# A hybrid attention block on one core: compression blocks, a q projection and the final gain moved to other places in the engines' queues

## The chip, the cores and the metric

The kernel runs on one core of a Trainium2 chip. That core has a matrix engine (TensorE, PE in the profile; PEld is its weight load), a vector engine (VectorE, DVE), a scalar engine (ScalarE, ACT), a general engine (GpSimd, POOL) and a queue that issues most transfers (SyncE, SP). Each engine works off its own queue in order, and they wait for each other by semaphores. The metric is the device time of one execution in microseconds (us); less is better. Three runs of the kernel before took 855.98, 856.62 and 858.67 us, so its median is 856.62 us.

## What is computed

The reference is one decoder block on x (512 tokens, 2048 features): a root-mean-square norm, one projection into queries, keys, values and gates, two kinds of attention, a SiLU gate, an output projection with a residual, and a last norm.

```python
h = _rmsnorm(x, norm_g[l]);  proj = h @ w_in[l]
kc = _compress(_rope(kca), cmp_k_pos, cmp_k_w1, cmp_k_w2)     # blocks of 32 tokens, stride 16
vc = _compress(vca, cmp_v_pos, cmp_v_w1, cmp_v_w2)            # silu((blocks + pos) @ w1) @ w2
o_cmp = attention(qa, kc, vc);  o_sel = selected blocks;  o_win = window of 512
o_a = g0 * o_cmp + g1 * o_sel + g2 * o_win                    # 8 heads of 128
o_b = banded attention, window 128, with sinks                # 16 heads of 64
x = x + concat(o_a * silu(za), o_b * silu(zb)) @ w_out
out = _rmsnorm(x, final_g)
```

`final_g` multiplies every column of the output, after each row has been divided by its root mean square.

## The kernel before

Every large product is made in three matmuls (`mm3`, L89): a float32 operand is split into a rounded high part and the low rest, and high by high, high by low and low by high are added up in PSUM. For a weight this split is `load_unit` (L60): SP issues a transfer of up to 128x1024 into `raw`, ACT rounds it to `whi` (L68), VectorE subtracts to get `wlo` (L69). `whi` and `wlo` have three buffers each, so ACT starts a new one only when the PE has finished with the one three units back. In the output projection `halves` and `split_to` (L632, L634) do the same.

The stages that the change touches, in order of time:

- **Opening and key loop** (L145, L241). The opening makes the keys and values that will be compressed (PSUM banks 0 to 3, `acc0`). The key loop over eight units of `w0[1]` makes the other keys (banks 4 to 7). Into its units, behind the `wlo` of each (`issue_after(last["lo"])` holds VectorE's part of a block behind that instruction), a list `work` puts one job each: `kv_evac` of the compressed keys (L179, three VectorE products with the rope tables and a sum), four `blocks_part` (L190) for them, and `kv_evac` of the compressed values (one VectorE product). A `blocks_part` is one VectorE sum with the position table into `ff` (L194), one ACT copy into the high half of F (L195) and one VectorE difference into the low half (L196).
- **First value loop** (L263): values from `w1s`, and the hidden layer of key compression from F0 (`compress_unit`, L199, which has a weight unit of its own and eight matmuls, L204 and L205).
- **Second value loop** (L292): nine rounds. Round u makes values and gates from `w2s` (408 columns; banks 4, 5, 2, 3) and, one round later, a unit of value compression from F1. F0 and F1 share one buffer (`tag="F"`), so the four `blocks_part` of F1 (L296) stand in round 0, when the PE has read F0 for the last time.
- **Evacuation of v** (L305): per tile of 128 tokens ACT scales and copies out of PSUM (L272, L273, L307), VectorE scales the gates (L308), POOL makes a low part (L274). Then the second compression layer, and then the heads. The first head begins with `proj(wz[0])`, two units of 24 matmuls of 512 columns, and goes on with the projection of its gate.
- **Output projection** (L684 to the end). The 2048 output columns go in four parts of 512. Part 0 is plain. Parts n = 1 to 3 work on sums and differences of quarter blocks: `product` with the operands named p, 22, 12, u, 21, q, w, where some weights are sums of two quarters. `summed` (L761) loads one quarter and adds the other to it with a transfer that POOL issues (L765); `add_to` (L769) adds a third quarter on VectorE (L772); `plus` (L784) adds results into `xs[n]`. The gain `final_g` is multiplied in by `times_g` (L663), a 128x512 product on POOL (L665), for parts 0 to 2; part 3 takes it in `final` (L670). Twelve such products run: those of part 1 and then of part 0 at the end of n = 1, those of part 2 within n = 2. A square with a row sum on ACT (`square`, L656) must have read a tile before its gain is multiplied in.

The order of the work on each engine is not written by hand: the program is made with `schedule_with_timeline_sim=True`, so a planner that simulates the engines takes instructions in the order of the program as their inputs and buffers come free, and `issue_after` puts bounds on it. The order that comes out is fixed at build time.

Of the kernel before, what the change touches and what calls it, by code (L numbers as in the profile page):

```python
# [10 lines left out]
F32 = mybir.dt.float32  # L11
# [22 lines left out]
def hybrid_block(ctx, tc, xT, xtm, w0, w1s, w2s, wz, wkb, wo0, wos, cw1, cw2, cpos, rope, tabs, sinks, gT, fg, out):  # L34
# [54 lines left out]
    def mm3(ps, ah, al, bh, bl, first, last, go_on=False):  # L89
        pe.matmul(ps, ah, bh, start=first, stop=False, skip_group_check=go_on)  # L90
        pe.matmul(ps, ah, bl, start=False, stop=False, skip_group_check=go_on)  # L91
        pe.matmul(ps, al, bh, start=False, stop=last, skip_group_check=go_on)  # L92
# [92 lines left out]
            dve.tensor_tensor(out=kvts[b][:, g, 0:S], in0=ps, in1=rstdb, op=ALU.mult)  # L185

    def blocks_tile(b):
        return s0.tile([P, 32, P], F32R, name=f"F{b}", tag="F")

    def blocks_part(Fb, b, g, half):  # L190
        ff = tmp("ff").rearrange("p (a b) -> p a b", b=32)
# [42 lines left out]
                    lo[:, j * width:(j + 1) * width], first, k == KT - 1 and (t % 2 == 1 or not shared))  # L234

    F0 = blocks_tile(0)
    work = [lambda g=g: kv_evac(0, g) for g in range(2)]
    work += [lambda g=g, half=half: blocks_part(F0, 0, g, half) for half in range(2) for g in range(2)]
    work += [lambda g=g: kv_evac(1, g) for g in range(2)]
    acc1 = [bank(4 + i) for i in range(4)]  # L240
    for u in range(KT // 2):  # L241
        hi, lo = load_unit(w0[1, :, u], 1024)
        with tc.issue_after(last["lo"]):
            work[u]()
        for j in range(2):
# [40 lines left out]

    for t in range(NQ):
        v_evac(t, 0, sacc[t])
    F1 = blocks_tile(1)
    sacc2 = [bank(t) for t in (4, 5, 2, 3)]  # L290
    vacc = bank(0)
    for u in range(9):  # L292
        if u < 8:
            tok_chunk(w2s, 408, [a[:, 0:408] for a in sacc2], False, u)
        if u == 0:
            for half in range(2):  # L296
                for g in range(2):
                    with tc.issue_after(last["lo"]):
                        blocks_part(F1, 1, g, half)
        else:  # L300
            compress_unit(F1, 1, u - 1, vacc)
        if u in (3, 5):
            with tc.issue_after(last["lo"]):
                k_evac(1, u // 5)
    for t in range(NQ):  # L305
# [21 lines left out]

    yt = [None] * 16
    ypair = []

    def proj(src):
        ps = psp.tile([P, S], F32, name="pj", tag="pj")
        for u in range(2):
            hi, lo = load_unit(src[:, u], 1024)
            for j in range(8):
                k = 8 * u + j
                mm3(ps, hi[:, j * P:(j + 1) * P], lo[:, j * P:(j + 1) * P], xh[:, k, :], xl[:, k, :], k == 0,
                    k == KT - 1)
        return ps

    def z_evac(ps):
        zr = wk.tile([P, S], F32, name="zr", tag="t2", bufs=1)
# [130 lines left out]

    for h in range(8):
        if h == 0:
            qh, ql = q_evac(proj(wz[0]), cosA, sinA)
        st = z_evac(proj(wz[8 + h]))
        cur = (qh, ql)
        attn_a(h, *cur, st)
        if h < 7:  # L480
            qh, ql = q_evac(proj(wz[h + 1]), cosA, sinA)
# [180 lines left out]

    def times_g(n, t):  # L663
        v = xs[n][t // 2][:, t % 2, :]
        pool.tensor_tensor(out=v, in0=v, in1=fgt[n // 2][:, (n % 2) * 512:(n % 2) * 512 + 512], op=ALU.mult)  # L665

    def pre_norm(t, k):
        dve.tensor_reduce(out=rs2[:, t, 0:1], in_=ssq[:, t, 0:k], axis=AX.X, op=ALU.add)
# [57 lines left out]
    for n in range(1, 4):  # L726
# [69 lines left out]
        if n < 3:  # L796
# [5 lines left out]
            product(bx, [halves(c) for c in ch], "u", True)  # L802
            plus(gg, gg, bx)
            plus(xa[1], xa[1], gg)
            r12 = [load(raw(), 1, g) for g in range(2)]
            if n == 1:
                load_gain()
# [1 line left out]
            plus(xb[1], xb[1], bb)  # L809
            plus(jj, jj, bb)  # L810
            plus(xb[0], xb[0], jj)
            add_to(ch, r12)
            product(bx, [halves(c) for c in ch], "q", False)
            plus(xb[0], xb[0], bx)
            for t in range(2):
                square(ssq[:, t, n + 1:n + 2], xs[n][0][:, t, :])
                times_g(n, t)
            s1 = summed(rw, 2, 3)
            product(bc, [halves(c) for c in s1], "w", True)
            plus(xa[1], xa[1], bc)  # L820
            for t in range(2, 4):
                square(ssq[:, t, n + 1:n + 2], xs[n][1][:, t - 2, :])
                times_g(n, t)
            if n == 1:
                for t in range(NQ):
                    times_g(0, t)
        else:
            by = psf1.tile([P, S], F32, name="oa", tag="oa").rearrange("p (t c) -> p t c", c=256)
            bxt = [bx, by]
            add_to(ch, r22)  # L830
            u5 = [halves(c) for c in ch]
            for t in range(2):
                product(bxt[t], u5, "u", True, (t,))
            for t in range(2):
                plus(xa[1][:, t, :], xa[1][:, t, :], bxt[t][:, t, :])
            plus(xa[1], xa[1], gg)
            r12 = [load(raw(), 1, g) for g in range(2)]
            product(bb, [halves(r) for r in r12], "21", False)
            plus(xb[1], xb[1], bb)
# [97 lines left out]
```

## Time and profile before

| | |
|---|---|
| median of 3 runs | 856.62 us |
| the profiled execution, its own time | 857.36 us |
| its span, first to last instruction | 855.3 us |
| busy PE | 835.8 us, 98% |
| busy VectorE / ACT / POOL | 591.1 / 405.1 / 112.6 us |
| mean granted PE clock | 0.994 |
| opening and key loop | 0 to 97 us |
| first / second value loop | 97 to 127 / 127 to 175 us |
| heads | 175 to about 700 us |
| output projection | about 670 to 850 us |

A busy PE is not a PE at its peak: matmuls overlap, and the end of one is modelled. Where the PE waits, though, the profile shows a gap and names what ended it. The rows of a timeline give start, duration, engine, line, and in brackets the idle time before the instruction with what it waited for.

### The profile page before, as it was taken

Reading aid. Unit: us, or ns where it says so; the run is one execution under the profiler, and the core shown is the slowest. Engines: PE = TensorE matmul, PEld = TensorE weight load, DVE = VectorE, ACT = ScalarE, POOL = GpSimd, SP = SyncE. Lnnn points to the kernel's source line nnn. Section 1 sums busy time; section 2 is a strip of 40 time slices with the busy share of each in tenths; the row PEclk is TensorE's granted clock in tenths of the full one; section 3 lists DMA queues with packets and bytes.
Section 4 is the critical chain, followed back from the end, with each engine's and each line's share of the span. In section 5 each row is a group of like instructions: output and inputs, shape, how many; then the busy total and the mean of one; then the engine's idle time right before and its main releaser. Section 6 shows DMA issues by size and latency. Waiting matters only on the chain.

```text
span 855.3 us, 12745 instructions
## 1 busy us (share of the span) xinstructions
PE 835.8 (98%) x4776; PEld 729.6 (85%) x4776; DVE 591.1 (69%) x1232; ACT 405.1 (47%) x845; POOL 112.6 (13%) x83
## 2 busy tenths in 40 slices
PE   9999998999999999999999999999999999899994
PEld 8788898978888888888888888888888788899994
DVE  6829476655675565775766877777767898767765
ACT  6723255443454443444443554544444737243536
POOL 4500001021110110110111201011101000430310
PEclk9999999999999999999999999999999999999998
DMA  9632274632212122121221221222222139696975
GB/s 324 207 120 87 86 227 134 192 107 91 75 50 75 58 66 74 60 65 61 89 74 51 92 79 54 90 82 72 68 83 75 49 99 310 160 276 162 260 164 197
DMA packets 33773, 101.40 MB, mean 119 GB/s; under 512 B 4016, under 2 KB 4016, under 8 KB 33712
## 3 DMA queue, kind: packets, MB, share of 16 engines
q1 hardware_dynamic: 30400, 90.90, 32.6%
q0 software_dynamic: 2016, 7.34, 5.0%
q10 hardware_dynamic: 1296, 2.36, 0.8%
q8 instruction: 37, 0.61, 0.3%
q14 instruction: 24, 0.20, 0.1%
HBM read 96.39 MB, written 4.19 MB: 118 GB/s over the span
## 4 chain that ended last, share of the span: by engine, by line
PE 88%; DMA 4%; DVE 3%; ACT 2%; issue 1%; SPq 0%; POOL 0%; ACTq 0%; DVEq 0%; POOLq 0%
PE pj L91 16%; PE pj L90 16%; PE pj L92 16%; PE bank L90 4%; PE bank L91 4%; PE bank L92 4%; PE sp L412 3%; PE oa L91 3%; PE oa L90 3%; PE oa L92 3%; DMA ch<-wos 2%; PE tp L447 2%; PE tp L582 1%; DMA raw<-wos 1%; PE op L456 1%
## 5 line engine op out<-in xcount | busy, mean ns | idle before, releaser
L90 PE MATMUL pj<-xh,whi 128*128 128x512 f32 x560 | 222.1, 397 | 0.7 <-ACT whi L68 0.7
L91 PE MATMUL pj<-xl,whi 128*128 128x512 f32 x560 | 222.3, 397 | 0.0
L92 PE MATMUL pj<-xh,wlo 128*128 128x512 f32 x560 | 221.8, 397 | 0.5 <-DVE wlo L69 0.5
L68 ACT ACTIVATE whi<-raw 128x1024 fp32r<-128x1024 f32 (+2 forms) x129 | 125.0, 972 | 159.9 <-PE pj L91 79.6
L69 DVE TENSOR_TENSOR wlo<-raw,whi 128x1024 fp32r<-128x1024 f32 (+2 forms) x130 | 151.4, 1170 | 68.9 <-ACT whi L68 67.9
L92 PEld LDWEIGHTS pj<-xh,wlo 128*128 128x128 f32 x560 | 105.4, 188 | 23.5 <-DVE wlo L69 1.0
L90 PEld LDWEIGHTS pj<-xh,whi 128*128 128x128 f32 x560 | 105.4, 188 | 22.9 <-ACT whi L68 1.0
L91 PEld LDWEIGHTS pj<-xl,whi 128*128 128x128 f32 x560 | 105.5, 188 | 22.5 <-issue 0.9
L353 POOL TENSOR_TENSOR t<-t,t 128x512 f32<-128x512 f32 x17 | 34.9, 2054 | 400.4 <-DVE t L97 384.9
L91 PE MATMUL oa<-wlo,yh 128*128 128x256 f32 (+1 forms) x208 | 62.3, 300 | 0.5 <-DVE wlo L634 0.5
L90 PE MATMUL oa<-whi,yh 128*128 128x256 f32 (+1 forms) x208 | 61.9, 299 | 0.6 <-ACT yh L629 0.6
L92 PE MATMUL oa<-whi,yl 128*128 128x256 f32 (+1 forms) x208 | 61.6, 299 | 0.0
L382 DVE TENSOR_TENSOR pl<-tp,ph 128x512 fp32r<-128x512 f32 x56 | 37.7, 685 | 34.3 <-ACT ph L381 34.1
L381 ACT ACTIVATE ph<-tp 128x512 fp32r<-128x512 f32 x56 | 32.4, 594 | 53.3 <-PE tp L447 43.5
L91 PE MATMUL bank<-wlo,xh 128*128 128x256 f32 (+1 forms) x128 | 40.1, 315 | 2.4 <-DVE wlo L69 2.4
L90 PEld LDWEIGHTS oa<-whi,yh 128*128 128x128 f32 x208 | 39.1, 188 | 2.1 <-ACT yh L629 0.8
L91 PEld LDWEIGHTS oa<-wlo,yh 128*128 128x128 f32 x208 | 39.2, 188 | 2.0 <-DVE wlo L634 0.7
L92 PEld LDWEIGHTS oa<-whi,yl 128*128 128x128 f32 x208 | 39.2, 188 | 1.4
L92 PE MATMUL bank<-whi,xl 128*128 128x256 f32 (+1 forms) x128 | 39.8, 313 | 0.0
L561 ACT ACTIVATE ttb<-ttb,mnb 128x256 f32<-128x256 f32 (+1 forms) x64 | 30.1, 471 | 20.2 <-DVE mnb L554 19.6
L90 PE MATMUL bank<-xh,whi 128*128 128x512 f32 x96 | 37.4, 400 | 0.0
L90 PE MATMUL bank<-whi,xh 128*128 128x256 f32 (+1 forms) x128 | 36.9, 316 | 0.5 <-ACT whi L68 0.5
(277 smaller groups left out, 1734.2 us busy)
## 6 DMA issues: line engine op xcount, KB each, us to landing
raw<-wz SPq DMA_DIRECT2D x64, 512.0 KB, 3.6
raw<-cw SPq DMA_DIRECT2D x16, 512.0 KB, 3.8
raw<-wos SPq DMA_DIRECT2D x14, 512.0 KB, 4.7
rw<-wos SPq DMA_DIRECT2D x12, 512.0 KB, 5.1
xr<-xT SPq DMA_DIRECT2D x16, 256.0 KB, 5.4
raw<-w SPq DMA_DIRECT2D x8, 512.0 KB, 3.7
raw<-wo SPq DMA_DIRECT2D x8, 512.0 KB, 3.7
raw<-w SPq DMA_DIRECT2D x15, 256.0 KB, 4.7
```

Source lines behind the costliest of these rows:

```text
L68: act.activation(hi[:, :width], raw[:, :width], AF.Copy)
L69: last["lo"] = dve.tensor_tensor(out=lo[:, :width], in0=raw[:, :width], in1=hi[:, :width].bitcast(F32), op=ALU.subtract).ins
L90: pe.matmul(ps, ah, bh, start=first, stop=False, skip_group_check=go_on)
L91: pe.matmul(ps, ah, bl, start=False, stop=False, skip_group_check=go_on)
L92: pe.matmul(ps, al, bh, start=False, stop=last, skip_group_check=go_on)
L353: pool.tensor_tensor(out=t1, in0=t1, in1=t2, op=ALU.add)
L381: act.activation(ph, tp, AF.Copy)
L382: dve.tensor_tensor(out=pl, in0=tp, in1=ph.bitcast(F32), op=ALU.subtract)
L412: pe.matmul(sp[:, a:b], qq[:, qs], kk[g][:, ko:ko + b - a], start=pi == 0, stop=pi == 2)
L447: pe.transpose(tp[:, e * 256 + i * P:e * 256 + i * P + P], views[2 * i + w][2][:, kt * P:(kt + 1) * P], ident)
L456: pe.matmul(oc, VL[:, kt, w, vs], ph[:, es], start=False, stop=False)
L561: act.activation(tv, tv, AF.Exp, bias=mn[:, e, v:v + 1], scale=-1.0, accum_out=dn[:, e, v:v + 1])
```

## The change

Three edits, all of order and place; the arithmetic is the same.

1. F0 and F1 get a buffer each. All eight `blocks_part` and all four `kv_evac` go into the key loop: unit 0 and 1 the two key evacuations, unit 2 both value evacuations, units 3 and 4 the four parts of F0, units 5, 6 and 7 one, two and one part of F1. The second value loop has eight rounds, and compression runs in the same round as the projection.
2. `proj(wz[0])` stands ahead of the evacuation of v, and the first head takes its result.
3. `times_g` runs on VectorE, each behind the last `wlo` that the program has issued, and at other places: part 0 in n = 2 (two tiles behind the sum that follows product u, two ahead of `add_to(ch, r12)`), parts 1 and 2 in n = 3 (two ahead of `add_to(ch, r22)`, four behind the sums that follow product u, two behind the loads for product 12).

```diff
     def blocks_tile(b):
-        return s0.tile([P, 32, P], F32R, name=f"F{b}", tag="F")
+        return s0.tile([P, 32, P], F32R, name=f"F{b}")
...
     F0 = blocks_tile(0)
-    work = [lambda g=g: kv_evac(0, g) for g in range(2)]
-    work += [lambda g=g, half=half: blocks_part(F0, 0, g, half) for half in range(2) for g in range(2)]
-    work += [lambda g=g: kv_evac(1, g) for g in range(2)]
+    F1 = blocks_tile(1)
+    kv = [lambda b=b, g=g: kv_evac(b, g) for b in range(2) for g in range(2)]
+    bp = [lambda Fb=Fb, b=b, g=g, half=half: blocks_part(Fb, b, g, half)
+          for b, Fb in enumerate((F0, F1)) for half in range(2) for g in range(2)]
+    work = [kv[:1], kv[1:2], kv[2:], bp[0:2], bp[2:4], bp[4:5], bp[5:7], bp[7:]]
...
         with tc.issue_after(last["lo"]):
-            work[u]()
+            for job in work[u]:
+                job()
...
-    F1 = blocks_tile(1)
...
-    for u in range(9):
-        if u < 8:
-            tok_chunk(w2s, 408, [a[:, 0:408] for a in sacc2], False, u)
-        if u == 0:
-            for half in range(2):
-                for g in range(2):
-                    with tc.issue_after(last["lo"]):
-                        blocks_part(F1, 1, g, half)
-        else:
-            compress_unit(F1, 1, u - 1, vacc)
+    for u in range(8):
+        tok_chunk(w2s, 408, [a[:, 0:408] for a in sacc2], False, u)
+        compress_unit(F1, 1, u, vacc)
...
+    q0 = proj(wz[0])
     for t in range(NQ):
         v_evac(t, 1, sacc2[t])
...
-            qh, ql = q_evac(proj(wz[0]), cosA, sinA)
+            qh, ql = q_evac(q0, cosA, sinA)
...
     def times_g(n, t):
         v = xs[n][t // 2][:, t % 2, :]
-        pool.tensor_tensor(out=v, in0=v, in1=fgt[n // 2][:, (n % 2) * 512:(n % 2) * 512 + 512], op=ALU.mult)
+        with tc.issue_after(last["lo"]):
+            dve.tensor_tensor(out=v, in0=v, in1=fgt[n // 2][:, (n % 2) * 512:(n % 2) * 512 + 512], op=ALU.mult)
...
             plus(xa[1], xa[1], gg)
+            if n == 2:
+                for t in range(2):
+                    times_g(0, t)
             r12 = [load(raw(), 1, g) for g in range(2)]
...
             plus(xb[0], xb[0], jj)
+            if n == 2:
+                for t in range(2, 4):
+                    times_g(0, t)
             add_to(ch, r12)
...
                 square(ssq[:, t, n + 1:n + 2], xs[n][0][:, t, :])
-                times_g(n, t)
...
                 square(ssq[:, t, n + 1:n + 2], xs[n][1][:, t - 2, :])
-                times_g(n, t)
-            if n == 1:
-                for t in range(NQ):
-                    times_g(0, t)
         else:
...
+            for t in range(2):
+                times_g(1, t)
             add_to(ch, r22)
...
             plus(xa[1], xa[1], gg)
+            for t in range(2):
+                times_g(1, 2 + t)
+                times_g(2, 2 + t)
             r12 = [load(raw(), 1, g) for g in range(2)]
...
             s2 = summed(raw, 0, 2)
+            for t in range(2):
+                times_g(2, t)
             plus(xa[1], xa[1], bc)
```

More of the change, by code (lines that the diff above doesn't have):

```diff
@@ L304, in hybrid_block, with proj @@
                 k_evac(1, u // 5)
+    def proj(src):
+        ps = psp.tile([P, S], F32, name="pj", tag="pj")
+        for u in range(2):
+            hi, lo = load_unit(src[:, u], 1024)
+            for j in range(8):
+                k = 8 * u + j
+                mm3(ps, hi[:, j * P:(j + 1) * P], lo[:, j * P:(j + 1) * P], xh[:, k, :], xl[:, k, :], k == 0,
+                    k == KT - 1)
+        return ps
+    q0 = proj(wz[0])
     for t in range(NQ):
@@ L329, in hybrid_block @@
     ypair = []
[L331 to L339, printed above, removed]
     def z_evac(ps):
```

## The prediction

> **What bounds the kernel now.** I read the page first (busy shares), then the list of waits for the PE alone, then the timeline around each wait.
>
> ```profile
> span 855.3 us, 12745 instructions
> PE 835.8 (98%) x4776; PEld 729.6 (85%) x4776; DVE 591.1 (69%) x1232; ACT 405.1 (47%) x845; POOL 112.6 (13%) x83
> ```
>
> The PE is busy for 98% of the span. The change takes no matmul away, so it can win only what the PE now loses in waits and in a lowered clock, and it loses wherever it makes the PE wait anew. The waits of the PE, each with total, count and longest in us:
>
> ```profile
> PE oa L91 <- DVE wlo L634: 3.1, 3, 2.4
> PE bank L91 <- DVE wlo L69: 2.4, 1, 2.4
> PE pj L90 <- ACT whi L68: 0.7, 1, 0.7
> PE pj L92 <- DVE wlo L69: 0.5, 1, 0.5
> PE bank L90 <- ACT whi L68: 0.5, 1, 0.5
> ```
>
> These five rows are nearly all of it, and each of the three edits stands beside one place: the two with `bank` (L69, L68) lie in the second value loop, the two with `pj` at the first q projection, and the 2.4 us of L634 in the output projection. What follows takes the places in turn.
>
> **Edit 1, the blocks of F1.** What VectorE and ACT do at the start of the second value loop, and the PE's wait there:
>
> ```profile
> 126.47 4.87 DVE L194 TENSOR_TENSOR ff<-kvt,pos 128x512 f32<-128x512 f32 x4
> 131.26 3.17 DVE L69 TENSOR_TENSOR wlo<-raw,whi 128x816 fp32r<-128x816 f32 x2
> 134.35 2.48 DVE L196 TENSOR_TENSOR F<-ff,F 128x512 fp32r<-128x512 f32 x4
> ```
>
> ```profile
> 132.81 0.46 PE L91 MATMUL bank<-wlo,xh 128*128 128x408 f32 x1 [2.44 <-DVE wlo L69]
> 133.11 0.35 PE L92 MATMUL bank<-whi,xl 128*128 128x408 f32 x1
> 133.30 0.34 PE L91 MATMUL bank<-wlo,xh 128*128 128x408 f32 x1
> ...
> 139.38 1.00 PE L90 MATMUL bank<-whi,xh 128*128 128x408 f32 x4 [0.46 <-ACT whi L68]
> ```
>
> ```profile
> 138.45 0.88 ACT L68 ACTIVATE whi<-raw 128x816 fp32r<-128x816 f32 x1 [2.81 <-PE bank L204]
> ```
>
> Four sums L194 take VectorE from 126.47 to 131.3, and the `wlo` that the PE needs is behind them: 2.44 us. The second wait is a consequence. The `whi` at 138.45 waits for a buffer that the PE gives back only with the compression matmuls (L204), which need F1, finished at 136.8: 0.46 us. With F1 built in the key loop both causes are gone, and compression of round 0 becomes work that the PE can take at once. Late next is the chain of key compression, since bank 3 of the new accumulators is taken by it until `kct` is read; it now also waits behind the F1 work, so I expect it earlier, not later. Gain: 2.9 us (2.44 + 0.46); at worst none of it, if evacuations on ACT keep `whi` late.
>
> What the key loop then has to carry: four L194 and four L196 more, and four ACT copies L195. Groups of VectorE from 60 to 98 us (busy, mean ns, idle before), and the copies (ns):
>
> ```profile
> L69 DVE TENSOR_TENSOR wlo<-raw,whi 128x1024 fp32r<-128x1024 f32 (+1 forms) x8 | 8.7, 1084 | 11.8 <-ACT whi L68 11.8
> L194 DVE TENSOR_TENSOR ff<-kvt,pos 128x512 f32<-128x512 f32 x4 | 4.0, 1046 | 0.0
> L196 DVE TENSOR_TENSOR F<-ff,F 128x512 fp32r<-128x512 f32 x4 | 2.5, 672 | 0.0
> ```
>
> ```profile
> L195 ACT ACTIVATE F<-ff x8: 620/636/641, 75.2 to 132.4; 128x512 fp32r<-128x512 f32 x8
> ```
>
> Four parts of F cost VectorE 4.0 + 2.5 = 6.5 us, and it idles 11.8 us in this stretch waiting for `whi`, while the PE waits nowhere. So the added 6.5 us cost nothing; the cover is that idle time, and what finds none of it is paid in full. There is one tight spot: the two value evacuations L185 (products of the size of L196, 2 x 0.67 = 1.3 us) now stand in unit 2, ahead of the `wlo` of unit 3, and that one is just in time:
>
> ```profile
> 69.13 1.23 DVE L69 TENSOR_TENSOR wlo<-raw,whi 128x1024 fp32r<-128x1024 f32 x1
> ```
>
> ```profile
> 70.50 0.63 PE L92 MATMUL bank<-xh,wlo 128*128 128x512 f32 x2
> 70.97 0.63 PE L92 MATMUL pj<-xh,wlo 128*128 128x512 f32 x2
> ```
>
> It ends at 70.36 and is read at 70.50. If L185 goes ahead, up to 1.3 us could open. But the planner has put L90 and L91 of four banks ahead of that L92, work without `wlo`, and the second half of the unit has four more such pairs (two matmuls from 70.50 to 70.97 make 0.23 us each, eight 1.9 us). I take 0 and keep 0 to 1.3 us for the range; a gain isn't to be had where the PE does not wait.
>
> **Edit 2, the q projection ahead of the evacuation of v.** ACT's queue at the end of the second value loop:
>
> ```profile
> 171.52 0.47 ACT L272 ACTIVATE vt<-bank,rstd 128x256 f32<-128x256 f32 x1 [1.20 <-PE bank L92]
> ...
> 174.57 1.10 ACT L68 ACTIVATE whi<-raw 128x1024 fp32r<-128x1024 f32 x1
> ```
>
> Evacuating copies fill ACT from 171.52 to 174.57 ahead of the first `whi` of the projection, and ACT had been idle for 1.20 us before them. The two `pj` waits, 0.7 and 0.5 us, are this `whi` and its `wlo`. Moved ahead, the `whi` needs only a buffer; with compression in the same round, the buffer three units back belongs to the compression unit before the last projection, freed 24 matmuls of 0.19 us (133.11 to 133.30), 4.6 us, and a compression unit before the loop's end. Gain 1.2 us. The evacuations then run under 48 matmuls of `pj`; at 0.23 us each that is 11 us of cover for a little over 3 us of ACT. What is queued behind: the value compression chain (two tiny PE steps), on which the freeing of the opening's buffers and so the evacuation of q0 hang. If its first PE step is put behind the whole of q0, the gate's projection, another 11 us, is its cover. I take 0; no row shows a wait there, the nearest are the two `pj` rows, so 0 to 1.2 us.
>
> **Edit 3, the gain on VectorE.** POOL, VectorE and PE around the largest wait:
>
> ```profile
> 729.22 6.99 POOL L665 TENSOR_TENSOR xs<-xs,late 128x512 f32<-128x512 f32 x4 [9.95 <-DMA late<-fg]
> ```
>
> ```profile
> 730.73 2.10 DVE L634 TENSOR_TENSOR wlo<-ch,whi 128x1024 fp32r<-128x1024 f32 x1 [2.83 <-ACT whi L633]
> 732.75 4.54 DVE L772 TENSOR_TENSOR ch<-ch,rw 128x1024 f32<-128x1024 f32 x2
> ...
> 737.81 2.35 DVE L634 TENSOR_TENSOR wlo<-ch,whi 128x1024 fp32r<-128x1024 f32 x2
> ```
>
> ```profile
> L772 DVE TENSOR_TENSOR ch<-ch,raw 128x1024 f32<-128x1024 f32 x2 | 2.4, 1218 | 0.0
> L785 DVE TENSOR_TENSOR late<-late,e 128x512 f32<-128x512 f32 x2 | 1.4, 683 | 0.0
> ```
>
> ```profile
> 736.26 0.38 PE L90 MATMUL oa<-whi,uh 128*128 128x256 f32 x1
> 739.08 0.39 PE L91 MATMUL oa<-wlo,uh 128*128 128x256 f32 x1 [2.43 <-DVE wlo L634]
> ```
>
> While POOL multiplies (729.22 to 736.2), a `wlo` takes 2.10 us and the two `ch` sums 4.54 us; the same sums take 1.22 us each a little later. Without POOL's products VectorE saves 0.9 + 2.1 = 3.0 us ahead of the `wlo` that the PE waits 2.43 us for, so that wait goes, with about half a microsecond to spare. And the PE pays for it twice (a stretch, its length, PE, PEld, VectorE, ACT and POOL busy, then the granted clock):
>
> ```profile
> 735.00:740.00 5.00, 2.57 (x19) 2.23 (x18) 5.00 (x5) 3.07 (x3) 2.00 (x2) 0.97 0.60 179
> 740.00:745.00 5.00, 5.00 (x33) 5.00 (x32) 2.77 (x5) 1.06 (x1) 0.96 (x2) 0.69 0.91 160
> ```
>
> At a clock of 0.69 it loses 5 x 0.31 = 1.55 us behind the wait. Gain 2.43 + 1.55 = 4.0 us; at least nothing. The Trainium skill (TensorE: Matmul & The Clock Gate, Part 1) has the clock fall only after an idle window of about 3.4 us, by which 2.43 us would not do it and edit 3 would be worth 2.4 us. The trace shows the fall here, and none behind the equally long wait at 132.81 (the PE steps there are 0.19 us again from 133.11 on), so I go by the rows.
>
> Against it stand twelve products on VectorE, 0.68 us each by L785: 8.2 us. Four are in n = 2:
>
> ```profile
> 775.00:815.00 40.00, 40.00 (x340) 40.00 (x339) 30.57 (x33) 18.24 (x24) 10.34 (x10) 1.00 0.86 235
> ```
>
> The PE never waits there and VectorE has 9.4 us free for 2.7 us; I take 0 (at worst 2.7 us). Eight are in n = 3, where VectorE still has holes:
>
> ```profile
> 818.27 0.42 DVE L785 TENSOR_TENSOR late<-late,oa 128x256 f32<-128x256 f32 x1 [1.08 <-PE oa L92]
> 820.19 1.23 DVE L634 TENSOR_TENSOR wlo<-raw,whi 128x1024 fp32r<-128x1024 f32 x1 [1.50 <-ACT whi L633]
> 821.33 2.35 DVE L772 TENSOR_TENSOR ch<-ch,raw 128x1024 f32<-128x1024 f32 x2
> ...
> 834.05 1.22 DVE L634 TENSOR_TENSOR wlo<-raw,whi 128x1024 fp32r<-128x1024 f32 x1 [3.51 <-ACT whi L633]
> ```
>
> Holes of 1.08, 1.50 and 3.51 us make 6.1 us for eight products of 5.4 us. The place that hurts is 821.33: the first `ch` sum frees the buffer into which the last weight quarter is loaded, and that transfer is what the `wlo` at 834.05, the last late one, hangs on. Four products (2.7 us) are issued between the sums after product u and that `add_to`. If all four go behind the `wlo` at 820.19, the end comes 2.7 us later. Their inputs are long done, so the planner can put them ahead, in the 2.6 us of the first two holes. I take 0, bounds 0 to 2.7 us.
>
> **The sum.** 2.9 + 1.2 + 4.0 = 8.1 us. Behind a wait the PE steps slowly once (133.11 after 132.81 is 0.30 us, against 0.19 to the next): 0.1 us for five waits is 0.5 us, an estimate. Together 8.6 us. The profiled execution took 857.36 us (span 855.3), so 848.8 us; it stands 0.7 us above the median of the runs, 856.62, so the forecast for the median is 848.0 us.
>
> **Rivals.**
>
> *The value loop keeps its wait* (chance 0.10). ACT's evacuations of the first value loop, not VectorE, would be what makes `whi` and `wlo` late at 130 us. For it: such copies cost 1.2 us at the end of the second loop, and the same kind stands here. Against: the row names `wlo`, and VectorE is full from 126.47. Time: 848.0 + 2.9 = 850.9 us.
>
> *The last part pays for the products* (0.12). The four products in n = 3 come behind 820.19: 848.0 + 2.7 = 850.7 us.
>
> *The clock falls for another reason* (0.06): then the dip stays and only the wait goes, 848.0 + 1.55 = 849.6 us. For it: the wait of 2.44 us at 132.81 brought no slow steps. Against: the 0.69 follows the 2.43 us at once. The idle window of the Trainium skill's rule above speaks for this one.
>
> *The key loop overflows, and the kernel is slower or the same* (0.17). If VectorE's queue puts the parts of F1 ahead of `wlo` where the lead is nil (as at 70.50) instead of in the late idle time, the PE pays 1.3 + 6.5 us, and up to 4 x 0.64 us for the copies that a part waits for, 10.3 us; a wait over 2.4 us brought a clock dip of 1.55 us, 11.9 us in all. 848.0 + 11.9 = 859.9 us. It decides from 8.6 us uncovered upwards. For it: `issue_after` orders only behind a `wlo`, not behind the next. Against: 11.8 us of idle VectorE. Half of it uncovered gives 854 us, no change.
>
> **How the numbers follow.** The forecast has 0.55 and its own range is 846.5 to 849.3 (1.5 us won beyond the sum, where small waits go with the large ones, or 1.3 us lost in the key loop). The three rivals that stay faster have 0.28 together. The range 846.5 to 853.5 us holds these, with two small losses at once, and leaves out the overflowing key loop (0.17) and little else. What a measurement of this kernel can tell from no change is about 0.3%, 2.6 us. Faster by more: 0.55 + 0.28 = 0.83. The overflow is split, 0.08 within and 0.09 slower.
>
> **What the profile of the changed kernel would show.** Edit 1: no wait of over a microsecond in the second value loop, eight L194 before 97 us, and no PE wait on `wlo` there. Edit 2: ACT's first `whi` of the projection ahead of the evacuating copies, no `pj` wait. Edit 3: no gain product on POOL, `ch` sums of 1.2 us throughout, no stretch with a clock under 0.95 ahead of the last matmuls, and the last late `wlo` no further from the last matmul than now. A PE wait on `wlo` before 97 us, or one at the last products longer than now, would prove the forecast wrong.

## The result and the profile after

The changed kernel takes 850.88 us (median of four runs, 850.5 to 851.69), and the kernel before, beside it on the same chip, 856.56 us (855.98 to 858.67). The ratio is 0.9931, with a 95% interval from 0.9912 to 0.9949: 0.7% faster. The forecast was 848.0 us with a range from 846.5 to 853.5. The profiled execution took 850.50 us against 857.36 before, and the spans are 848.7 and 855.3 us. Runs of one kernel lie several us apart (849.81 to 854.04 us in eleven later runs of the changed kernel), so effects of about 1 us are read below from the stages of profiled executions and not from the medians.

The head of the page of the changed kernel:

```profile
span 848.7 us, 12742 instructions
PE 833.0 (98%) x4776; PEld 727.2 (86%) x4776; DVE 597.1 (70%) x1244; ACT 404.7 (48%) x845; POOL 94.1 (11%) x71
```

VectorE has the twelve gain products more (x1244 against x1232) and POOL has them less (x71 against x83). The PE is bound as before. Its waits (total, count and longest, in us):

```profile
PE pj L90 <- DVE t L97: 1.2, 1, 1.2
PE bank L143 <- DVE still L140: 1.1, 1, 1.1
PE bank L92 <- DVE wlo L69: 0.9, 1, 0.9
PE bank L90 <- ACT whi L68: 0.8, 2, 0.4
PE oa L90 <- ACT yh L625: 0.6, 1, 0.6
PE bank L205 <- DVE wlo L69: 0.2, 1, 0.2
```

The waits of 2.4 us and the two on `pj` at the first q projection are gone. Two rows of more than 0.2 us are new: 1.2 us behind L97, which is the rope of a query in the heads, and 0.9 us on a `wlo` in L92. (The 1.1 us of L143 in the opening and the 0.6 us of `yh` stand in the list of before too.)

Where the time went is read from the start of the first matmul of each stage in the timeline. The table has the length of each stage in us and its difference to before; "after, again" is a second profiled execution of the changed kernel, and the columns "1", "2" and "3" are kernels with one edit alone, of which the next section tells.

| stage | before | after | after, again | 1 alone | 2 alone | 3 alone |
|---|---|---|---|---|---|---|
| opening | 50.59 | +0.38 | -0.06 | +1.35 | -0.26 | +0.42 |
| key loop | 46.05 | +1.21 | +1.22 | +1.21 | +0.01 | -0.08 |
| first value loop | 30.16 | +0.06 | +0.02 | +0.04 | +0.04 | +0.02 |
| second value loop, to the first q matmul | 48.92 | -3.99 | -4.04 | -4.04 | -0.92 | -0.30 |
| from there to the end of part 0 (heads) | 543.36 | +1.35 | +1.32 | -0.08 | +1.93 | -0.06 |
| n = 1 | 44.29 | -4.42 | -4.42 | +1.29 | -1.72 | -4.42 |
| n = 2 | 39.87 | 0.00 | 0.00 | +0.01 | 0.00 | 0.00 |
| n = 3, to the last matmul | 41.63 | -1.88 | -1.88 | -0.41 | -0.94 | -1.42 |
| last matmul to the end | 10.39 | +0.73 | +0.59 | 0.00 | -0.03 | +1.29 |
| sum | 855.25 | -6.56 | -7.25 | -0.63 | -1.89 | -4.55 |

The opening differs between executions whatever the edit, and so does n = 1 (below). The other entries repeat to 0.15 us between the two executions of the changed kernel. The border between the second value loop and the heads is not the same with edit 1 as without: seven matmuls of the compression, 0.12 us each, then come behind the first q matmul instead of ahead of it (264 matmuls in the loop's row instead of 271), so that 0.8 us of its -3.99 is moved and not won. The two rows added up are free of that: -2.64 us with all edits, -4.12 with edit 1 alone, +1.01 with edit 2 alone and -0.36 with edit 3 alone.

*Second value loop.* VectorE there, in the changed kernel's timeline:

```profile
130.68 1.23 DVE L69 TENSOR_TENSOR wlo<-raw,whi 128x1024 fp32r<-128x1024 f32 x1 [2.70 <-ACT whi L68]
132.06 1.30 DVE L69 TENSOR_TENSOR wlo<-raw,whi 128x816 fp32r<-128x816 f32 x1 [0.16 <-ACT whi L68]
```

```profile
131.96 0.39 PE L205 MATMUL bank<-wlo,F 128*128 128x256 f32 x1 [0.17 <-DVE wlo L69]
139.73 1.01 PE L90 MATMUL bank<-whi,xh 128*128 128x408 f32 x4 [0.41 <-ACT whi L68]
```

The 4.87 us of L194 that stood ahead of a `wlo` are gone, VectorE now waits for ACT, and the PE waits 0.17 us where it waited 2.44. The smaller wait, 0.46 us, has stayed (0.41 us at 139.73).

*Key loop.* VectorE and PE in the changed kernel:

```profile
65.29 1.28 DVE L185 TENSOR_TENSOR kvt<-bank,rstdb 128x512 f32<-128x512 f32 x2
...
70.72 2.36 DVE L69 TENSOR_TENSOR wlo<-raw,whi 128x1024 fp32r<-128x1024 f32 x2
```

```profile
72.01 0.72 PE L92 MATMUL bank<-xh,wlo 128*128 128x512 f32 x2 [0.92 <-DVE wlo L69]
```

The two evacuations of the compressed values (1.28 us) do stand ahead of the `wlo` of unit 3. It begins at 70.72 instead of 69.13, and the PE waits 0.92 us for it.

*Heads.* VectorE and PE at the first query of the second kind of attention:

```profile
482.81 0.68 DVE L97 TENSOR_TENSOR t<-pj,sinA 64x512 f32<-64x512 f32 x1
```

```profile
483.55 0.51 PE L90 MATMUL pj<-xh,whi 128*128 128x512 f32 x1 [1.24 <-DVE t L97]
```

The rope reads the query's projection out of PSUM (`pj`, two buffers), and its last read ends at 483.49; the next projection but one needs that buffer and waits 1.24 us.

*Output projection.* The stretch with the dip of the clock, in the changed kernel (length, PE, PEld, VectorE, ACT and POOL busy, granted clock), and VectorE ahead of it:

```profile
735.00:740.00 5.00, 5.00 (x44) 5.00 (x44) 3.73 (x5) 2.12 (x2) 1.75 (x2) 1.00 0.75 161
740.00:745.00 5.00, 5.00 (x44) 5.00 (x43) 5.00 (x6) 2.09 (x2) 0.00 (x0) 1.00 1.02 254
```

```profile
729.35 1.23 DVE L630 TENSOR_TENSOR wlo<-ch,whi 128x1024 fp32r<-128x1024 f32 x1 [2.44 <-ACT whi L629]
730.49 2.35 DVE L769 TENSOR_TENSOR ch<-ch,rw 128x1024 f32<-128x1024 f32 x2
```

The `wlo` takes 1.23 us (2.10 before) and the two `ch` sums 2.35 us (4.54 before). The PE is busy throughout and the clock stays at 1.00.

### The profile page after: what moved, and what is told of

Its sections match the earlier page's. It is cut to its first block, busy times and chain, and to the rows that moved or that the text cites. A ratio compares the mean times of both kernels' runs of the same rounds, so it can differ in the third digit from the quotient of the medians.

```text
span 848.7 us, 12742 instructions
## 1 busy us (share of the span) xinstructions
PE 833.0 (98%) x4776; PEld 727.2 (86%) x4776; DVE 597.1 (70%) x1244; ACT 404.7 (48%) x845; POOL 94.1 (11%) x71
## 3 DMA queue, kind: packets, MB, share of 16 engines
q10 hardware_dynamic: 1296, 2.36, 0.8%
## 4 chain that ended last, share of the span: by engine, by line
PE 90%; DMA 3%; DVE 2%; ACT 2%; issue 1%; POOL 0%; ACTq 0%; SPq 0%; DVEq 0%; POOLq 0%
PE pj L91 17%; PE pj L92 17%; PE pj L90 17%; PE oa L90 4%; PE oa L92 4%; PE oa L91 4%; PE bank L92 4%; PE bank L90 4%; PE bank L91 4%; PE sp L408 3%; PE tp L443 2%; DMA xr<-xT 1%; PE tp L578 1%; DMA raw<-wos 1%; PE op L452 1%
## 5 line engine op out<-in xcount | busy, mean ns | idle before, releaser
L92 PE MATMUL pj<-xh,wlo 128*128 128x512 f32 x560 | 221.9, 397 | 0.0
L92 PEld LDWEIGHTS pj<-xh,wlo 128*128 128x128 f32 x560 | 105.4, 188 | 22.4
L92 PE MATMUL oa<-whi,yl 128*128 128x256 f32 (+1 forms) x208 | 61.6, 299 | 0.0
L92 PEld LDWEIGHTS oa<-whi,yl 128*128 128x128 f32 x208 | 39.2, 188 | 1.4
L92 PE MATMUL bank<-whi,xl 128*128 128x256 f32 (+1 forms) x128 | 39.9, 314 | 0.0
L91 PE MATMUL bank<-xl,whi 128*128 128x512 f32 x96 | 37.4, 394 | 0.0
```

## The experiments

In the timeline rows of all kernels the number in brackets is the idle time ahead of the instruction and what ended it; the line numbers shift a little from kernel to kernel.

### Each edit alone

The kernel before with the hunks of one edit only, as the diff of the change has them. The heart of each, in this order:

```diff
+    work = [kv[:1], kv[1:2], kv[2:], bp[0:2], bp[2:4], bp[4:5], bp[5:7], bp[7:]]
...
+    for u in range(8):
+        tok_chunk(w2s, 408, [a[:, 0:408] for a in sacc2], False, u)
+        compress_unit(F1, 1, u, vacc)
```

```diff
+    q0 = proj(wz[0])
     for t in range(NQ):
         v_evac(t, 1, sacc2[t])
```

```diff
-        pool.tensor_tensor(out=v, in0=v, in1=fgt[n // 2][:, (n % 2) * 512:(n % 2) * 512 + 512], op=ALU.mult)
+        with tc.issue_after(last["lo"]):
+            dve.tensor_tensor(out=v, in0=v, in1=fgt[n // 2][:, (n % 2) * 512:(n % 2) * 512 + 512], op=ALU.mult)
```

> The kernel before with edit 1 alone (F1 in the key loop). Against 856.6 us of the kernel before. Theory 'each edit acts at its own place': the second value loop gives back 2.2 us, the key loop loses 1.2 us at unit 3 (the wait on wlo that the changed kernel shows at 72 us), so about 855.5 us, with no new PE wait in the heads and the waits at the first q projection (1.8 us with the slow steps) and at 739 us (4.4 us with the low clock) kept. Rival 'the planner's order shifts further down': the new 1.4 us PE wait at the change from the first to the second kind of heads appears here too, and the time is about 857 us.

> The kernel before with edit 2 alone (first q projection ahead of the evacuation of v). Theory 'own place': the two pj waits go, 1.8 us, so 854.8 us, all else as before, the wait at 739 us and the low clock behind it among it. Rival 'order shifts further down': the 1.4 us wait near 480 us appears here, 856.2 us.

> The kernel before with edit 3 alone (gain products on VectorE at the new places). Theory 'own place': n = 1 gives 4.4 us, the waits at the last products 1.9 us, the end after the last matmul takes 0.7 us, so about 851.0 us. Rival 'the last products' waits went because of the shifted order from the early edits': they stay here, 852.5 us.

The ratios to the kernel before: edit 1 alone 0.9969 (0.9956 to 0.9982), 854.87 us; edit 2 alone 1.0008 (0.9992 to 1.0024), 857.12 us; edit 3 alone 0.9968 (0.9951 to 0.9984), 854.27 us; the kernel before took 857.47 us beside them. Edit 1 came out near what was expected, 855.5 us. The other two are longer than both of their numbers (854.8 and 856.2 for edit 2, 851.0 and 852.5 for edit 3); 0.9 us of it has the kernel before too on this chip, and the rest is not explained. Runs of one kernel spread by 4 to 7 us here (851.49 to 857.57 with edit 3 alone), and the profiled executions stand off the medians, at 856.74, 855.14 and 852.49 us.

The stages are in the table above. Edit 1 has the whole gain of the second value loop, the `pj` waits included, and the whole loss of the key loop. Edit 2 alone brings 0.92 us in the loop, of which edit 3 alone, which changes nothing there, has 0.30 too, and loses 1.93 us in the heads, as the rival had it. Its waits:

```profile
PE oa L91 <- DVE wlo L635: 2.6, 2, 2.4
PE bank L91 <- DVE wlo L69: 2.1, 1, 2.1
PE pj L90 <- DVE t L97: 1.6, 2, 1.2
...
PE pj L92 <- DVE wlo L69: 0.5, 1, 0.5
```

A `pj` wait of 0.5 us is still there, and 1.6 us of waits on L97 are new. ACT shows why its own gain is small (edit 2 alone, then edit 1 alone):

```profile
171.00 0.47 ACT L272 ACTIVATE vt<-bank,rstd 128x256 f32<-128x256 f32 x1 [1.38 <-PE bank L92]
...
173.45 1.09 ACT L68 ACTIVATE whi<-raw 128x1024 fp32r<-128x1024 f32 x1
```

```profile
169.06 2.21 ACT L68 ACTIVATE whi<-raw 128x1024 fp32r<-128x1024 f32 x2 [3.06 <-issue]
172.76 0.47 ACT L275 ACTIVATE vt<-bank,rstd 128x256 f32<-128x256 f32 x1 [1.49 <-PE bank L92]
```

With edit 2 alone ACT still evacuates ahead of the third `whi`, in spite of the order of the program. With edit 1 alone two `whi` in a row, one of them the projection's first, stand ahead of the evacuation, although the program has them behind it. So the place in the program did not decide. That a free buffer did is read from the code: with eight rounds instead of nine, a `whi` buffer is free before the loop's last unit is done.

### Edits 1 and 3, without 2

```diff
-    q0 = proj(wz[0])
     for t in range(NQ):
         v_evac(t, 1, sacc2[t])
...
-            qh, ql = q_evac(q0, cosA, sinA)
+            qh, ql = q_evac(proj(wz[0]), cosA, sinA)
```

> The changed kernel with edit 2 undone (edits 1 and 3 alone). Theory 'edit 1 alone already frees the buffer for the first projection's whi, and edit 2 only brings the 1.4 us wait near 480 us': no pj wait at the first projection, no wait near 480 us, 849.5 us against 850.9 us of the changed kernel. Rival 'edit 2 is what removed the pj waits': they come back, 1.8 us, and the time is 850.9 + 1.8 - 1.4 = 851.3 us.

850.96 us, ratio 0.9932 (0.9905 to 0.9958): the time of all three edits, and nearer to the rival's 851.3 us than to the 849.5 of the theory. The waits decide for the theory all the same: none on `pj` is left. In the profiled execution (span 847.5 us) the second value loop gains the same 4.00 us, the heads lose nothing (-0.06 us), and the key loop loses 1.22 us. Edit 2 adds nothing to edit 1 in the loop and is the cause of the wait in the heads, which are 1.41 us longer with it (544.71 us against 543.30). How it brings this about is argued, not shown: the projection that edit 2 puts ahead is work with which the PE would otherwise fill the heads' holes. With all three edits the first score matmul of the second kind of attention comes at 481.19 us, with edits 1 and 3 at 473.18 (475.95 before). Before, projection matmuls stand between these scores; in the changed kernel none does, and the chain to the next query goes through ACT's copy, POOL's difference, VectorE's copies and the rope, with less projection left to run beside it.

### The value evacuations in a later unit

```diff
-    work = [kv[:1], kv[1:2], kv[2:], bp[0:2], bp[2:4], bp[4:5], bp[5:7], bp[7:]]
+    work = [kv[:1], kv[1:2], [], bp[0:2], bp[2:4], kv[2:], bp[4:6], bp[6:]]
```

This was made in the changed kernel, and then in the kernel with edits 1 and 3.

> The changed kernel with the two value evacuations moved from unit 2 of the key loop to unit 5 (and the parts of F1 to units 6 and 7, two each). Theory 'the two L185 ahead of the wlo of unit 3 cost 1.2 us': the PE wait at 72 us goes and the time is 849.7 us against 850.9 us of the changed kernel. Rival 'the key loop is short of VectorE altogether': the wait only moves to a later unit, 850.9 us or more.

> Edits 1 and 3, with the two value evacuations in unit 5 of the key loop instead of unit 2, and without edit 2. Both corrections together, if they add up: 850.9 - 1.1 - 1.4 = 848.4 us, with no PE wait over 1 us behind the opening. If the order shifts again, a wait of the size of the one near 480 us stands elsewhere and the time is 849.8 us.

All three edits with it: 849.96 us, ratio 0.9915 (0.9904 to 0.9927); the key loop is +0.02 us, the heads keep their +1.35 us. Edits 1 and 3 with it: 849.27 us, ratio 0.9911 (0.9887 to 0.9935), profiled span 846.4 us; key loop -0.09 us, heads -0.06 us, second value loop -4.03 us, n = 1 -4.42 us. The median lies between the two numbers expected, 848.4 and 849.8; the profiled execution took 848.23 us. The waits of this last kernel:

```profile
PE bank L143 <- DVE still L140: 1.1, 1, 1.1
PE bank L90 <- ACT whi L68: 0.6, 2, 0.4
PE oa L90 <- ACT yh L624: 0.6, 1, 0.6
PE bank L90 <- ACT xh L116: 0.3, 1, 0.3
PE bank L205 <- DVE wlo L69: 0.2, 1, 0.2
```

So the 1.2 us of the key loop were the two L185 ahead of one `wlo` and nothing else: the blocks of F1 cost nothing there. With both losses taken away no wait above 0.6 us is left behind the opening. The intervals of all these kernels overlap with that of the changed kernel, so the times alone do not tell which is the fastest; the stages show what each has lost.

### Is it POOL that slows VectorE?

Three kernels. In the first, the kernel before with part 0's four products alone on VectorE, in n = 2 as in the change:

```diff
+        if n == 0:
+            with tc.issue_after(last["lo"]):
+                dve.tensor_tensor(out=v, in0=v, in1=fgt[0][:, 0:512], op=ALU.mult)
+            return
         pool.tensor_tensor(out=v, in0=v, in1=fgt[n // 2][:, (n % 2) * 512:(n % 2) * 512 + 512], op=ALU.mult)
```

in the second, the changed kernel with the products on POOL at the new places, without the bound:

```diff
-        with tc.issue_after(last["lo"]):
-            dve.tensor_tensor(out=v, in0=v, in1=fgt[n // 2][:, (n % 2) * 512:(n % 2) * 512 + 512], op=ALU.mult)
+        pool.tensor_tensor(out=v, in0=v, in1=fgt[n // 2][:, (n % 2) * 512:(n % 2) * 512 + 512], op=ALU.mult)
```

in the third, the changed kernel with 40 memsets of a scratch tile on POOL in n = 1, which write to SBUF and read nothing:

```diff
         ch = summed(chain, 0, 2)
+        if n == 1:
+            with tc.issue_after(last["pool"]):
+                for _ in range(40):
+                    pool.memset(scr, 0.0)
```

> The kernel before with the four products of part 0 alone on VectorE in n = 2; those of parts 1 and 2 stay on POOL where they were. Theory 'the four products on POOL at 729 us are the whole cost in n = 1': n = 1 gives 4.4 us as with all of edit 3. For the last products: if their waits (1.9 us before) went because products of part 1 and 2 on VectorE changed the order in n = 3, they stay here and the time is 852.6 us; if they went for another reason they go here too, 851.2 us.

> The changed kernel with the twelve products at their new places in the program but on POOL, without a bound on their order. Theory 'the engine, not the place in the program, is what counts': POOL is idle, so the planner pulls the four products of part 0 ahead to where they were, the ch sums take 2.3 us again, the PE wait of 2.4 us comes back and with the low clock the time is about 855 us. Rival 'the place counts': no such wait, 851 us.

> The changed kernel with 40 memsets of a 128x512 scratch tile on POOL in n = 1, behind the accumulating transfers: POOL is busy there but reads nothing from SBUF. Theory (VectorE with two SBUF inputs is slowed by POOL reading SBUF): the ch sums stay at 1.22 us and wlo at 1.23 us beside the memsets, and the time is that of the changed kernel, 850.9 us within 1.5. Rival (any busy POOL slows VectorE): ch sums of about 2.3 us beside them, and a PE wait near 738 us again, 853 us or more.

*POOL at the new places*: 855.08 us, ratio 0.9972 (0.9955 to 0.9989). POOL and VectorE:

```profile
726.86 7.97 POOL L661 TENSOR_TENSOR xs<-xs,late 128x512 f32<-128x512 f32 x4 [9.79 <-DMA late<-fg]
```

```profile
727.66 1.57 DVE L630 TENSOR_TENSOR wlo<-ch,whi 128x1024 fp32r<-128x1024 f32 x1 [1.41 <-ACT whi L629]
729.15 4.52 DVE L768 TENSOR_TENSOR ch<-ch,rw 128x1024 f32<-128x1024 f32 x2
```

Without the bound the planner draws part 0's products forward to n = 1, as soon as the gain has landed. The sums take 4.52 us again, and the PE waits 1.16 us at 735.97. The median is as expected; the wait is not the 2.4 us expected, and no low clock follows it, in a profiled execution (852.38 us) that was the fastest of ten and in which the sums could begin early (below). So the new place in the program does nothing by itself. Whether POOL's products, held in n = 2 by a bound, would do as well as VectorE's was not run.

*Memsets*: one run, 852.51 us. POOL and VectorE:

```profile
717.65 15.68 POOL L797 MEMSET scr<- 128x512 f32 x26
```

```profile
728.62 1.23 DVE L630 TENSOR_TENSOR wlo<-ch,whi 128x1024 fp32r<-128x1024 f32 x1 [1.99 <-ACT whi L629]
729.76 2.35 DVE L770 TENSOR_TENSOR ch<-ch,rw 128x1024 f32<-128x1024 f32 x2
```

POOL writes without a break from 717.65 to 733.3, and beside it the `wlo` takes 1.23 us and the sums 2.35 us for two, the durations without any POOL work. n = 1 has its 39.87 us. In this one execution a POOL busy with writing does not slow VectorE; POOL's products, which read two operands from SBUF, do. That is what the Trainium skill states (SBUF — State Buffer, § Who interferes with whom): a VectorE instruction with two SBUF inputs contends with a GpSimd instruction that reads SBUF, not with one that only writes it. The total is 0.1 us above the upper end of what was expected, for another reason: 2.27 us more than in the changed kernel between the start of n = 3 and the last matmul, where a weight sum landed late (ACT's `whi` of it begins at 819.14 instead of 816.74) and the PE waited 0.9 and 0.4 us.

*Part 0 alone*: 854.3 us, ratio 0.9965 (0.9947 to 0.9982), longer than both numbers expected. In the profiled execution, the slowest of ten (856.55 us), POOL makes no product near n = 1 and the sums take 2.36 us, yet n = 1 is 2.72 us longer than in the changed kernel. ACT and VectorE:

```profile
729.80 1.06 ACT L633 ACTIVATE whi<-ch 128x1024 fp32r<-128x1024 f32 x1 [2.64 <-DMA ch<-wos]
733.99 1.06 ACT L633 ACTIVATE whi<-ch 128x1024 fp32r<-128x1024 f32 x1 [3.13 <-DMA ch<-wos]
```

```profile
736.22 2.36 DVE L776 TENSOR_TENSOR ch<-ch,rw 128x1024 f32<-128x1024 f32 x2
```

Here the second accumulating transfer into `ch` is late: its `whi` begins 13.4 us after n = 1 does, and the PE waits twice for 0.9 us. Over the profiled executions of all kernels this `whi` comes 9.1 to 13.4 us after the part's beginning. Where it came by 10.4 us and POOL made no product, n = 1 took 39.87 us (after: 10.2 us). So there are two causes of a wait in n = 1: POOL's products, and a transfer whose landing varies from run to run. Part of that variation stands in POOL's rows. POOL issues the two transfers when the plain quarters have landed in `ch` (the second 0.3 us behind that landing, in all thirteen executions). The issue in the latest case and in the earliest (part 0 alone, where n = 1 begins at 720.54, and POOL at the new places, where it begins at 717.44) stands in these rows:

```profile
721.03 1.90 POOL L769 DMA_DIRECT2D ch<-wos  x2 [72.54 <-DVE xs L714]
715.16 1.90 POOL L761 DMA_DIRECT2D ch<-wos  x2 [69.82 <-DVE ql L630]
```

It comes 0.5 us behind the beginning of the part in the one and 2.3 us ahead of it in the other. That is 2.8 us of the 4 us by which the landings differ; from issue to landing the second transfer took 9.7 to 11.8 us. With the transfer so late, this run does not decide whether part 0's products are the whole cost in n = 1.

### The load of the gain behind other loads

Edits 1 and 3 with the value evacuations later, and `load_gain()` in n = 1 moved; beside it the changed kernel once more, without an edit.

```diff
             r12 = [load(raw(), 1, g) for g in range(2)]
-            if n == 1:
-                load_gain()
...
             s1 = summed(rw, 2, 3)
+            if n == 1:
+                load_gain()
```

> Edits 1 and 3 with the value evacuations in unit 5 and without edit 2 (849.27 us before), and with the load of final_g moved in n = 1 behind the loads that follow product u, so that 1 MB stands later in SP's queue. Theory: the accumulating transfers at the beginning of n = 1 share the DMA engines with that load, and their late landing is the run-varying cause of waits in n = 1; then they land within 9 us of the part's beginning, the runs lie closer together, and the median is 848.3 us. Rival: the transfers are late for other reasons (the loads of the weights themselves); then nothing changes, 849.3 us within 0.5.

> The changed kernel once more, on the chip of the next run, as its neighbour for comparison. 850.9 us within 1 us. Theory (the losses that edits 1 and 2 brought are fixed by the order of instructions): the key loop has its PE wait of 0.9 to 1.1 us near 72 us and the heads one of 1.2 to 1.4 us near 483 us, in this execution too. Rival (they are accidents of one execution): one of them is absent.

848.81 us, ratio 0.9907 (0.988 to 0.9933), against 850.60 us for the changed kernel on the same chip (0.9933, 0.9915 to 0.9951). Against the 849.27 us that this kernel took on another chip with the load at its old place it is no change that can be told, and the runs do not lie closer together (847.77 to 851.26 us, against 848.23 to 851.81). The profiled execution speaks against the theory (ACT):

```profile
723.38 1.06 ACT L628 ACTIVATE whi<-ch 128x1024 fp32r<-128x1024 f32 x1 [1.35 <-DMA ch<-wos]
727.38 1.06 ACT L628 ACTIVATE whi<-ch 128x1024 fp32r<-128x1024 f32 x1 [2.94 <-DMA ch<-wos]
```

The second `whi` comes 12.0 us after the part's beginning (715.42), not within 9, and n = 1 takes 41.11 us with a wait of 0.9 us. The load of the gain, now issued 17 us into the part, is not what makes the transfer late: from issue to landing it took 11.8 us here, as long as anywhere. What does stays open, but for the late issue shown above. The changed kernel's second execution has both new waits, 0.9 and 1.2 us, at the same places: they belong to the order of the instructions.

## Why the prediction was right, and where it was off

Faster was right, the range held, and the three large losses went where the prediction said; one of them went by another edit than it said. The forecast's own range, 846.5 to 849.3 us, did not hold: the 850.88 us lie where two rivals stood (850.9 and 850.7), and neither of them came about. Nor was the range kept by a small error: two terms that were put at zero cost 2.6 us, and the range was wide enough for it. And the sign that the prediction itself named as proof against it, a PE wait on `wlo` before 97 us, did come, the 0.92 us at 72.01 (and 0.17 us on a `wlo` in the second value loop, where there was to be none).

The sum was 8.6 us where the profiled executions differ by 6.56 (7.25 in the second one). Step by step:

- **Second value loop, 2.9 us, and the `pj` waits, 1.2 us.** Together 4.1 us were forecast (0.4 more with the slow restarts of four waits), and 4.06 to 4.12 us came in loop and heads together, where edit 1 was made and edit 2 was not. The cause of the second half was wrong: the gain was booked on edit 2, and edit 1 alone has it. The prediction even names the reason, the buffer that is free earlier with compression in the same round, but takes it as a help for edit 2 where it did all the work. The 0.46 us at 139.38 was called a consequence and is not: with F1 long ready the wait is still 0.41 us.
- **Key loop, 0 with bounds 0 to 1.3.** The 6.5 us of F1 did cost nothing. The tight spot named at unit 3 cost 1.21 us, almost its upper bound. The step that failed is "I take 0": the PE had 0.14 us to spare at that `wlo`, and the cover counted on, four more pairs of `pj` and `bank` matmuls without `wlo`, was not drawn ahead to fill it. The planner's order was the order of before with a gap in it.
- **Edit 2's follow-on, 0 with bounds 0 to 1.2.** It cost 1.41 us against the same kernel without it, and not at the value compression chain, where the prediction looked, but 300 us later in the heads. The step failed because it asked only what is queued behind the moved projection, and not where the projection had been of use as filler.
- **n = 1, 4.0 us.** 4.42 us came: the wait of 2.43 us, 1.7 us by the clock and 0.3 us that a wait costs beyond its length, for which the sum had 0.1 in its last term. The 1.55 us of the prediction are a little short, because its stretch of 0.69 begins at 740.00 and the clock had fallen at 739.70 (last section). The rival "the clock falls for another reason" did not come about here. But the price of the clock is not always paid: with edit 2 alone the wait of 2.4 us was there and the stretch behind it ran at 1.00, so that n = 1 was only 2.70 us longer than without a wait; with edit 1 alone the clock fell again.
- **The products in n = 2 and n = 3, 0 with bounds to 2.7.** n = 2 is unchanged to 0.01 us. n = 3 did not pay, it won 1.88 us to the last matmul and gave 0.6 to 0.7 us back behind it (1.3 in the kernels with edit 3 and without edit 2; why is open). That was not in the sum. ACT at the end, before and after:

```profile
836.65 1.28 ACT L673 ACT_TABLE_LOAD   x1
...
839.09 1.04 ACT L633 ACTIVATE whi<-ch 128x1024 fp32r<-128x1024 f32 x1
```

```profile
830.57 1.04 ACT L629 ACTIVATE whi<-ch 128x1024 fp32r<-128x1024 f32 x1
831.63 1.28 ACT L670 ACT_TABLE_LOAD   x1
```

Before, the last `whi` stood behind a table load and the squares, and the PE waited for it and its `wlo`, and ahead of that for the `wlo` of 834.05:

```profile
835.33 0.39 PE L91 MATMUL oa<-wlo,yh 128*128 128x256 f32 x1 [0.49 <-DVE wlo L634]
835.56 0.28 PE L92 MATMUL oa<-whi,yl 128*128 128x256 f32 x1
...
840.19 0.50 PE L90 MATMUL oa<-whi,qh 128*128 128x256 f32 x2 [0.44 <-ACT whi L633]
...
841.45 0.39 PE L91 MATMUL oa<-wlo,qh 128*128 128x256 f32 x1 [0.17 <-DVE wlo L634]
```

After, that `whi` comes ahead of the table load, and none of the three waits is left. The list of before had them (two in the 3.1 us of L634), and the prediction did not ask what would become of them. In all eight kernels with the products of parts 1 and 2 on VectorE the last `whi` comes ahead of the table load, and in all five with them on POOL behind it, those with the products at their new places and with part 0's alone moved among them. n = 3 took 39.75 to 40.40 us in seven of the eight (42.02 with the memsets, where a weight sum was late) and 40.70 to 41.63 us in the five. Why the planner orders ACT otherwise is open.

The two zeros that became 1.21 and 1.41 us make 2.62 us; the unexpected gain in n = 3 (1.88 - 0.73 = 1.15 us) took less than half of it back, and that was luck. Of the overflow of the key loop, the rival on the other side, only the first term came, the 1.3 us of L185 ahead of a `wlo`, a tenth of its 11.9 us; the 6.5 us of F1, the copies and the low clock did not.

## What to carry to other kernels

Where a `wlo` or any other operand is just in time (here 0.14 us), book work put ahead of it at its full length, not at zero: 1.28 us put there cost 1.21 us, and moving the same two instructions three units on cost nothing. Before pulling independent work of the busiest engine forward, look for the place where it now fills a hole, however far away that is. And test edits of one change singly: one of the three did nothing that the first had not done already, and without it and with one list entry moved the profiled execution spans 846.4 us, against 848.7 and 848.0 with all three edits as they stand (the medians, 849.27 against 850.88 and 850.60, are too close to tell).

## What the runs showed of the hardware

*The clock.* It falls behind some waits of the PE of 2.1 to 2.9 us and not behind others of the same length. Of seven such waits in five profiled executions three were followed by a fall, the shortest of them 2.14 us long. Stretches behind the three waits, with the granted clock as the third number from the end: the kernel before, behind 2.43 us at 739.08; edit 1 alone, behind 2.91 us at 738.86; part 0 alone, in the second value loop, behind 2.14 us at 132.80:

```profile
739.70:743.10 3.40, 3.40 (x19) 3.40 (x18) 2.79 (x4) 0.00 (x0) 1.26 (x2) 0.50 0.85 163
740.21:743.62 3.41, 3.41 (x18) 3.41 (x18) 2.06 (x3) 0.52 (x1) 0.88 (x1) 0.50 1.00 172
133.46:136.87 3.41, 3.41 (x13) 3.34 (x13) 3.37 (x5) 1.22 (x2) 0.00 (x0) 0.50 0.79 189
```

Two without a fall: edit 2 alone, behind 2.42 us at 739.67, and the kernel before in the second value loop, behind 2.44 us at 132.81:

```profile
740.00:745.00 5.00, 5.00 (x45) 5.00 (x43) 4.29 (x6) 1.06 (x2) 1.63 (x2) 1.00 0.85 181
133.50:137.00 3.50, 3.50 (x22) 3.50 (x21) 3.50 (x6) 1.11 (x2) 0.00 (x0) 1.00 0.79 204
```

Each fall came 0.6 to 1.4 us behind the end of the wait and was of the same size: half the clock for 3.4 us, which costs a busy PE 1.7 us. The Trainium skill (TensorE: Matmul & The Clock Gate, Part 1) has a window of 3413 ns that runs freely; that it runs freely fits a fall that hits one wait and spares a longer one, and the length of the three falls is that of the window, while a wait well under the window's length was enough here.

*The price of a wait.* A wait costs the PE 0.2 to 0.35 us more than the length that the profile gives: 0.92 us became 1.21 in the key loop, 1.24 became 1.41 in the heads, and in n = 1, without a fall of the clock, 0.89, 1.16 and 2.42 us became 1.24, 1.43 and 2.70. The profile counts a wait from the end of the last matmul, 0.28 us behind its start, where the next one would have started after 0.12; and the first step behind the wait is slow (835.33 to 835.56 in the rows of the kernel before, 0.23 us instead of 0.12). Together that is 0.27 us, of which the prediction had the second part alone.

*Accumulating transfers.* The landing of the same transfer in n = 1 varied by 4.0 us between thirteen executions, 9.0 to 13.1 us behind the part's beginning, and where POOL made no product there the PE waited with its `whi` at 12.0 us (0.9 us) and at 13.4 us (twice 0.9 us). Whether this and the falls of the clock are what spreads the runs (853.65 to 861.44 us over 16 runs of the kernel before on one chip) is not shown.
